# First loads in a fixed order on one queue with tiny transfers between them, four free places for weights, and eight products of zeros at the start of a two-layer trunk

## The chip, the core and the metric

One core of a Trainium2 chip runs the whole program. The engines are named as the profile names them: PE (TensorE, matrix products; PEld is its weight load), DVE (VectorE), ACT (ScalarE), POOL (GpSimd) and SP (SyncE, which issues all DMAs here). The metric is the device time of one execution in microseconds (us). It is the median of several runs. The span of the profile is the time from the first to the last instruction of one profiled execution, and it is a little shorter than the time of that execution.

## What is computed

The reference is a trunk of two layers on 256 positions of width 1024, in float32. Layer 0 mixes positions by a gated unit, layer 1 by attention with 16 heads; each is followed by a layer norm, a gated feed-forward part with a short convolution, and another layer norm. Only the very start is touched by the change:

```
def chunked_gmlp(x, w_in, ln_g, ln_b, w_s, b_s, w_out):
    z = jax.nn.gelu(x @ w_in)
    u, v = jnp.split(z, 2, axis=-1)
    v = layer_norm(v, ln_g, ln_b)
...
    sv = jnp.einsum('gts,bnsgc->bntgc', w, v) + b_s.T[None, None, :, :, None]
    return (u * sv.reshape(B, S, GMLP_WIDTH)) @ w_out
```

The kernel computes the half `v` first (weights `a_v`), then `u` (`a_u`), then the product with `w_out` (`a_out`). Everything after that is the same in both kernels but for small shifts in order.

## The kernel before

All weights come from DRAM in chunks of 128 x 2048 float32, which is 1 MB each. A chunk is loaded into one of two buffers `raw` and is split there: ACT writes a rounded copy `whi` (line 338) and DVE the remainder `wlo` (line 344), in halves of 1024 columns; both kinds have room for five chunks. The input `x` is treated in the same way: its transposed form `xT` is loaded to a place in `ff` and split into the two parts of `xt`. A product of two float32 matrices is then three products on PE: rounded by rounded, rounded by remainder, remainder by rounded (`mms`, line 326).

The first stage is `a_v`: four chunks, each with the weights of two of the eight input blocks k. For each k there are two row tiles t and two column halves, so 2 x 2 x 3 = 12 products of 512 columns, 96 in all. For k = 0 to 3 both row tiles take turns (48 products); then row tile 0 takes k = 4 to 7, then row tile 1. The second stage `a_u` has eight groups of 24 products of 256 columns, and mixed in are the small products of `spatial` (tiles `twos<-ff`), which need the normed `v`.

The order of the work is not written out. The code records operations with their dependences, and `Plan.emit` runs a model of the engines and issues each engine's instructions in the order of that model. Loads all go on SP's queue, in the order that the model gives; the first ones carry a rank, which the model uses as their due time. SP takes its instructions strictly in order, and one that waits for a buffer holds up all that stand behind it.

At the start chunk 0 is loaded in three pieces (512, 512 and 1024 columns) and chunk 1 in two (1024 each), mixed with `xT` in pieces of 1, 1, 2 and 4 blocks. `xT` lies in DRAM as partition, row tile, k, column, so a load of one block reads two runs of 128 elements in each partition. Chunks 2 and 3 go into the same two `raw` buffers as chunks 0 and 1, so each load waits until DVE has read the last half of the chunk before it. `lnrow` is a buffer of one chunk's size that holds the rows of a layer norm; its first use is the norm of `v`.

## Time and profile before

| what | value |
|---|---|
| median of 3 runs | 573.56 us |
| lowest and highest | 572.23 and 574.41 us |
| the profiled execution | 573.82 us |
| its span in the profile | 572.1 us |
| PE busy | 557.8 us (98%) |
| DVE busy | 459.9 us (80%) |
| ACT busy | 356.0 us (62%) |
| chain that ended last | PE 91%, DMA 4%, DVE 2%, SP's queue 1% |

PE is the engine of this kernel: what it does not spend on products is the start, the end and the few stretches where it waits. The groups of rows further down show the start closely. In the rows of the order of time, several instructions of one group that follow each other stand in one row (x2, x4), with the start of the first and the time from there to the end of the last; in square brackets stands how long the engine had been idle and what ended it. An idle time that ends with "DMA raw<-in_a_v" ends when such a load has landed.

### The profile page before, as it was taken

How to read it: one execution, taken by the hardware profiler on the slowest of the kernel's cores; microseconds unless marked ns; L12 is line 12 of the kernel's file. 1: busy time of each engine (PE TensorE's matmuls, PEld its weight loads, DVE VectorE, ACT ScalarE, POOL GpSimd, SP SyncE). 2: the span in 40 equal slices, each digit the busy share in tenths (PEclk: the TensorE clock that was granted, in tenths of full speed). 3: DMA queues.
4: the chain of work that ended last, by engine and by line, in shares of the span. 5: the costliest groups of instructions: out<-in, count | busy, mean ns of one | idle time of the engine just before them, and what ended most of it. 6: DMA issues, size and time to landing. Idle time of an engine off the chain costs nothing.

```text
span 572.1 us, 8555 instructions
## 1 busy us (share of the span) xinstructions
PE 557.8 (98%) x3226; PEld 482.7 (84%) x3226; DVE 459.9 (80%) x857; ACT 356.0 (62%) x652; POOL 11.5 (2%) x17
## 2 busy tenths in 40 slices
PE   6999999999999999999999999999999999999994
PEld 4799888888888878888899998788888888888884
DVE  4589989999999998467858767589989999997426
ACT  5474558776677786335569666367867767785300
POOL 0020010000000000001000000000000000000001
PEclk9999999999999999999999999999999999999998
DMA  7887644537554657652666542506456446566302
GB/s 259 307 300 288 257 147 158 211 147 255 187 220 149 221 224 263 227 212 92 221 221 236 207 156 84 222 1 211 158 215 226 183 186 214 196 245 231 144 1 73
DMA packets 20133, 110.93 MB, mean 194 GB/s; under 512 B 2251, under 2 KB 6268, under 8 KB 7676
## 3 DMA queue, kind: packets, MB, share of 16 engines
q1 hardware_dynamic: 20092, 110.39, 52.9%
q8 instruction: 25, 0.41, 0.3%
q14 instruction: 16, 0.13, 0.1%
HBM read 109.31 MB, written 1.07 MB: 193 GB/s over the span
## 4 chain that ended last, share of the span: by engine, by line
PE 91%; DMA 4%; DVE 2%; SPq 1%; ACT 0%; issue 0%; DVEq 0%
PE twos L326 52%; PE bank L326 38%; DMA raw<-in_a_v 2%; DMA raw<-in_a_u 2%; DVE wlo L344 1%; PE bank L332 1%; PE twos L332 1%; SPq L355 1%; ACT whi L338 0%; DVE x L348 0%; DVE ff L348 0%; DVE stat L494 0%; DVEq L964 0%; DVE stat L497 0%; DVE stat L499 0%
## 5 line engine op out<-in xcount | busy, mean ns | idle before, releaser
L344 DVE TENSOR_TENSOR wlo<-raw,whi 128x1024 fp32r<-128x1024 f32 (+1 forms) x212 | 228.9, 1103 | 39.2 <-ACT whi L338 38.6
L338 ACT ACTIVATE whi<-raw 128x1024 fp32r<-128x1024 f32 (+1 forms) x212 | 194.8, 954 | 58.7 <-DMA raw<-in_f_dn 24.5
L326 PE MATMUL twos<-xt,whi 128*128 128x512 f32 x640 | 222.2, 394 | 0.0
L326 PE MATMUL twos<-xt,wlo 128*128 128x256 f32 x640 | 177.3, 277 | 0.0
L326 PEld LDWEIGHTS twos<-xt,whi 128*128 128x128 f32 x640 | 120.0, 188 | 27.7
L326 PE MATMUL bank<-whi,rr 128*128 128x512 f32 x432 | 135.1, 391 | 0.0
L326 PEld LDWEIGHTS twos<-xt,wlo 128*128 128x128 f32 x640 | 120.2, 188 | 0.1
L326 PEld LDWEIGHTS bank<-whi,rr 128*128 128x128 f32 x432 | 81.1, 188 | 17.8 <-issue 1.0
L326 PE MATMUL bank<-wlo,rr 128*128 128x512 f32 x216 | 84.1, 389 | 0.0
L326 PE MATMUL bank<-xt,whi 128*128 128x256 f32 x384 | 71.8, 288 | 0.0
L348 DVE SCALAR_TENSOR_TENSOR ff<-ff,convc 128x254 f32<-128x254 f32 (+1 forms) x160 | 69.7, 478 | 0.5 <-ACT ff L338 0.2
L326 PEld LDWEIGHTS bank<-xt,whi 128*128 128x128 f32 x384 | 59.6, 191 | 2.0 <-issue 1.0
L338 ACT ACTIVATE ff<-twos 128x512 f32<-128x512 f32 (+1 forms) x56 | 31.0, 567 | 46.3 <-PE twos L326 43.9
L326 PE MATMUL bank<-xt,wlo 128*128 128x256 f32 x192 | 54.2, 282 | 0.0
L326 PEld LDWEIGHTS bank<-wlo,rr 128*128 128x128 f32 x216 | 40.6, 188 | 8.2
L338 ACT ACTIVATE ff<-ff,convc 128x256 f32<-128x256 f32 x80 | 45.6, 592 | 1.9 <-DVE ff L344 1.4
L326 PE MATMUL twos<-whi,xt 128*128 128x512 f32 x128 | 42.0, 396 | 0.0
L344 DVE TENSOR_TENSOR ff<-twos,ff 128x512 f32<-128x512 f32 (+1 forms) x48 | 30.9, 645 | 13.2 <-ACT ff L338 12.3
L338 ACT ACTIVATE ff<-bank,lncol 128x128 f32<-128x128 f32 x48 | 18.8, 458 | 30.5 <-PE bank L332 30.5
L326 PEld LDWEIGHTS bank<-xt,wlo 128*128 128x128 f32 x192 | 36.7, 191 | 0.0
L348 DVE SCALAR_TENSOR_TENSOR x<-x,bank 128x512 f32<-128x512 f32 x16 | 11.0, 686 | 27.4 <-PE bank L326 27.4
L326 PEld LDWEIGHTS twos<-whi,xt 128*128 128x128 f32 x128 | 24.1, 188 | 4.7
(70 smaller groups left out, 480.4 us busy)
## 6 DMA issues: line engine op xcount, KB each, us to landing
raw<-in_f_up SPq DMA_DIRECT2D x44, 1024.0 KB, 4.8
raw<-in_f_dn SPq DMA_DIRECT2D x22, 1024.0 KB, 4.8
raw<-in_b_qk SPq DMA_DIRECT2D x8, 1024.0 KB, 4.8
lnrow<-in_lnrow SPq DMA_DIRECT2D x5, 1024.0 KB, 5.8
raw<-in_a_u SPq DMA_DIRECT2D x4, 1024.0 KB, 4.7
raw<-in_a_out SPq DMA_DIRECT2D x4, 1024.0 KB, 5.1
raw<-in_b_v SPq DMA_DIRECT2D x4, 1024.0 KB, 4.8
raw<-in_b_o SPq DMA_DIRECT2D x4, 1024.0 KB, 4.8
```

The costliest lines, as they stand in the source:

```text
L326: nc.tensor.matmul(o, l, x, start=start, stop=stop)
L332: nc.tensor.transpose(o, x, ident.ap)
L338: plan.op("act", ns, lambda: nc.scalar.activation(o, x, func, **kw), r, w, table=table)
L344: dve(70 + 1.04 * flat(x), lambda: nc.vector.tensor_tensor(o, x, y, op=op), r, w)
L348: lambda: nc.vector.scalar_tensor_tensor(o, x, s, y, op0=op0, op1=op1), r, w)
L355: plan.op("sp", nbytes / 360.0, lambda: nc.sync.dma_start(o, src), r, w, nbytes=nbytes, rank=rank)
```

## The change

Five things are changed, all of them in the first stage.

- `xT` lies in DRAM so that the part of each partition that one load takes is one run: 256 elements for one block where there were two runs of 128. Both row tiles of up to two blocks are now split by one instruction each.
- Chunk 2 goes to a place in `ff` that is free at that time and chunk 3 to `lnrow`; neither waits for a `raw` buffer any more. The first norm's rows and `wsT` are loaded after these have been split.
- Ranked loads are issued strictly in the order of rank. Ahead of those with rank 5, 7, 9 and 10 stands a transfer of 16 elements from a loaded piece to `scratch`. It waits until the piece has landed, and since it stands on the same queue, what is behind it waits with it. The pieces are the first 512 columns of chunk 0, its second half, the first half of chunk 1 and its second half.
- DVE fills 512 columns with zeros at the start, and PE multiplies them eight times, into a bank that is used later.
- The twelve products of k = 0 are ordered so that both row tiles use a rounded half before its remainder, in the first column half and then in the second.

```diff
+WARM = 8
...
+                if e == "sp" and ranked:
+                    c = [x for x in c if x[1] is ranked[-1]]
...
+    FIRST = {0: [(0, 512, 0), (512, 1024, 2), (1024, 2048, 4)], 1: [(0, 1024, 6), (1024, 2048, 7)],
+             2: [(0, 2048, 9)], 3: [(0, 2048, 10)]}
...
     XFIRST = ((0, 1, 1), (1, 1, 3), (2, 2, 5), (4, 4, 8))
+
+    EARLY = {2: lambda: place("ff", HALF + KT * S, CH), 3: rowring.new}
+
+
+    HOLD = {5: (0, 0), 7: (0, SUB), 9: (1, 0), 10: (1, SUB)}
+    scratch = sb.tile([1, 16 * len(HOLD)], F32, name="scratch")
+    loaded, gates = {}, []
+
+    def hold(rank):
+        i, at = HOLD[rank]
+        g = Buf(scratch[:, 16 * len(gates):16 * len(gates) + 16])
+        load(g.ap, loaded[i].ap[:1, at:at + 16], [g], [(loaded[i], [at // 256])], nbytes=64, rank=rank - 0.5)
+        gates.append(g)
...
-        raw = raws.new()
+        raw = loaded[i] = EARLY.get(i, raws.new)()
         cuts = FIRST.get(i, [(0, CH, None)])
         for s, e, rank in cuts:
-            load(raw.ap[:, s:e], a[name][c, :, s:e], [(raw, range(s // 256, e // 256))], rank=rank)
+            if rank in HOLD:
+                hold(rank)
+            load(raw.ap[:, s:e], a[name][c, :, s:e], [(raw, range(s // 256, e // 256))],
+                 gates[-1:] if i <= CHUNKS else (), rank=rank)
...
+    zeros, idle = place("rr", 0, HALF), bank()
+    dve(480, lambda: nc.vector.memset(zeros.ap.bitcast(F32), 0.0), (), [zeros])
+    for _ in range(WARM):
+        mms([(idle.ap, zeros.ap[:, :P], zeros.ap, True, True)], [zeros], [idle], fill=True)
...
+        def first_step():
+
+            (hi, lo), x = sub("a_v", 0, 0), [at(0, t) for t in range(NT)]
+            for p in range(2):
+                for part, w in ((0, hi), (1, hi), (0, lo)):
+                    for t in range(NT):
+                        o, n, b = pieces[t][p]
+                        mms([(b.ap, x[t][part], w.ap[:, o:o + n], part == 0 and w is hi, False)],
+                            x[t][2][part:part + 1] + [(w, range(o // 256, (o + n) // 256))], [b])
+            plan.tick()
...
-        "xT": f(x.reshape(NT, P, KT, P).transpose(3, 0, 2, 1)),
+        "xT": f(x.reshape(NT, P, KT, P).transpose(3, 2, 0, 1).reshape(P, KT * S)),
```

On SP's queue, before, behind the first two 512-column pieces of chunk 0 and the first two blocks of `xT`, the loads stand like this (`raw_85` and `raw_86` are the two `raw` buffers):

```order
L355 DMA raw_85<-in_a_v 128x1024
L355 DMA ff<-in_xT 128x2x256
L355 DMA raw_86<-in_a_v 128x1024 x2
L355 DMA ff<-in_xT 128x2x512
L355 DMA raw_85<-in_a_v 128x2048
L355 DMA raw_86<-in_a_v 128x2048
L355 DMA lnrow_90<-in_lnrow 128x2048
L355 DMA raw_85<-in_a_u 128x2048
L355 DMA raw_86<-in_a_u 128x2048
```

And now at the same place:

```order
L361 DMA raw_85<-in_a_v 128x1024
L361 DMA scratch<-raw_85 1x16x1
L361 DMA ff<-in_xT 128x512
L361 DMA raw_86<-in_a_v 128x1024
L361 DMA scratch<-raw_85 1x16x1
L361 DMA raw_86<-in_a_v 128x1024
L361 DMA ff<-in_xT 128x1024
L361 DMA scratch<-raw_86 1x16x1
L361 DMA ff<-in_a_v 128x2048
L361 DMA scratch<-raw_86 1x16x1
L361 DMA lnrow_90<-in_a_v 128x2048
L361 DMA raw_85<-in_a_u 128x2048
```

Four tiny transfers stand between the loads, chunks 2 and 3 go to `ff` and `lnrow`, and the first load of `lnrow`'s own rows has moved behind two chunks of `a_u`.

On PE, before, the program starts with the products of k = 0 (`whi_65` and `wlo_75` are the parts of its weights, the four banks are the two row tiles by the two column halves):

```order
L326 MATMUL bank_107<-whi_65,xt 128x512
L326 MATMUL bank_107<-wlo_75,xt 128x512
L326 MATMUL bank_107<-whi_65,xt 128x512
L326 MATMUL bank_108<-whi_65,xt 128x512
L326 MATMUL bank_108<-wlo_75,xt 128x512
L326 MATMUL bank_108<-whi_65,xt 128x512
```

And now:

```order
L332 MATMUL bank_107<-rr 128x512 x8
L332 MATMUL bank_108<-whi_65,xt 128x512
L332 MATMUL bank_110<-whi_65,xt 128x512
L332 MATMUL bank_108<-whi_65,xt 128x512
L332 MATMUL bank_110<-whi_65,xt 128x512
L332 MATMUL bank_108<-wlo_75,xt 128x512
L332 MATMUL bank_110<-wlo_75,xt 128x512
```

The eight products of zeros stand first, and four products with `whi_65` come ahead of the first with `wlo_75`.

On PE in the second stage, before, the first products of `spatial` (`twos<-ff`) stand at the end of the third group of `a_u` (bank_109):

```order
L326 MATMUL bank_109<-xt,whi_65 128x256 x2
L326 MATMUL bank_109<-xt,wlo_75 128x256
L326 MATMUL twos_105<-ff 128x128 x2
L326 MATMUL twos_106<-ff 128x128 x2
L326 MATMUL bank_110<-xt,whi_66 128x256 x2
```

And now they stand behind the first three products of the third group (bank_110 there):

```order
L332 MATMUL bank_109<-xt,whi_74 128x256 x2
L332 MATMUL bank_109<-xt,wlo_84 128x256
L332 MATMUL bank_110<-xt,whi_65 128x256 x2
L332 MATMUL bank_110<-xt,wlo_75 128x256
L332 MATMUL twos_105<-ff 128x128 x2
L332 MATMUL twos_106<-ff 128x128 x2
L332 MATMUL bank_110<-xt,whi_65 128x256 x2
```

They have moved forward by 21 of the group's 24 products.

## Rows read from the trace of the kernel before

**Rows 1.** The page: the span, and the engines' shares of the chain that ended last.

```profile
span 572.1 us, 8555 instructions
...
PE 91%; DMA 4%; DVE 2%; SPq 1%; ACT 0%; issue 0%; DVEq 0%
```

**Rows 2.** All waits of PE in the whole span: total us, times, longest.

```profile
PE bank L326 <- DVE xt L361: 5.0, 1, 5.0
PE bank L326 <- DVE wlo L344: 1.3, 2, 0.8
PE twos L326 <- DVE ff L348: 0.2, 1, 0.2
```

**Rows 3.** PE in order of time, first stage: start us, time us, what. The last row is the first product of the second stage.

```profile
5.00 0.77 PE L326 MATMUL bank<-whi,xt 128*128 128x512 f32 x1 [5.00 <-DVE xt L361]
5.85 0.79 PE L326 MATMUL bank<-wlo,xt 128*128 128x512 f32 x1
...
8.57 0.63 PE L326 MATMUL bank<-wlo,xt 128*128 128x512 f32 x1
...
11.13 0.54 PE L326 MATMUL bank<-wlo,xt 128*128 128x512 f32 x1
11.51 0.62 PE L326 MATMUL bank<-whi,xt 128*128 128x512 f32 x2
...
13.35 0.39 PE L326 MATMUL bank<-wlo,xt 128*128 128x512 f32 x1
...
14.03 0.39 PE L326 MATMUL bank<-wlo,xt 128*128 128x512 f32 x1
...
19.02 0.61 PE L326 MATMUL bank<-whi,xt 128*128 128x512 f32 x2
20.21 0.50 PE L326 MATMUL bank<-wlo,xt 128*128 128x512 f32 x1 [0.58 <-DVE wlo L344]
...
24.04 0.50 PE L326 MATMUL bank<-wlo,xt 128*128 128x512 f32 x1 [0.76 <-DVE wlo L344]
...
32.11 0.40 PE L326 MATMUL bank<-xt,whi 128*128 128x256 f32 x2
```

**Rows 4.** Stretches: busy us (instructions) of PE, PEld, DVE, ACT and POOL, then the granted clock, the share of the DMA engines and GB/s.

```profile
5.00:7.00 2.00, 1.92 (x4) 1.22 (x5) 1.69 (x4) 0.63 (x1) 0.00 (x0) 1.00 0.85 240
...
10.00:11.00 1.00, 1.00 (x4) 0.81 (x3) 0.90 (x2) 0.54 (x3) 0.00 (x0) 1.00 1.01 412
...
35.00:40.00 5.00, 5.00 (x44) 5.00 (x43) 5.00 (x12) 2.66 (x4) 1.71 (x2) 1.00 0.89 344
```

**Rows 5.** ACT in order of time: the splits of `raw` and `xT` and the loads that ended its waits.

```profile
4.29 0.63 ACT L338 ACTIVATE whi<-raw 128x512 fp32r<-128x512 f32 x1 [2.21 <-DMA raw<-in_a_v]
5.46 0.63 ACT L338 ACTIVATE whi<-raw 128x512 fp32r<-128x512 f32 x1 [0.54 <-DMA raw<-in_a_v]
7.46 0.51 ACT L338 ACTIVATE xt<-ff 128x128 fp32r<-128x128 f32 x2 [1.37 <-DMA ff<-in_xT]
8.94 1.15 ACT L338 ACTIVATE whi<-raw 128x512 fp32r<-128x512 f32 x2 [0.97 <-DMA raw<-in_a_v]
10.56 0.72 ACT L338 ACTIVATE xt<-ff 128x256 fp32r<-128x256 f32 x2 [0.46 <-DMA ff<-in_xT]
11.85 2.42 ACT L338 ACTIVATE whi<-raw 128x512 fp32r<-128x512 f32 x4 [0.57 <-DMA raw<-in_a_v]
14.41 1.15 ACT L338 ACTIVATE xt<-ff 128x512 fp32r<-128x512 f32 x2
17.84 2.01 ACT L338 ACTIVATE whi<-raw 128x1024 fp32r<-128x1024 f32 x2 [2.27 <-DMA raw<-in_a_v]
21.67 2.01 ACT L338 ACTIVATE whi<-raw 128x1024 fp32r<-128x1024 f32 x2 [1.83 <-DMA raw<-in_a_v]
```

**Rows 6.** DVE in order of time at the start.

```profile
0.87 0.06 DVE L421 MEMSET nhalf<- 128x1 f32 x1 [0.87 <-PEq L961]
4.63 0.36 DVE L361 CAST xt<-ff 128x128 fp32r<-128x128 f32 x2 [3.70 <-DMA ff<-in_xT]
5.11 0.68 DVE L344 TENSOR_TENSOR wlo<-raw,whi 128x512 fp32r<-128x512 f32 x1
```

**Rows 7.** SP's queue in order of time: when a load was issued. The last row is a piece of the chain that ended last: the fourth `a_u` chunk, from its issue to its landing.

```profile
3.16 0.60 SPq L355 DMA_DIRECT2D raw<-in_a_v  x1
...
10.93 4.51 SPq L355 DMA_DIRECT2D raw<-in_a_v  x2
...
35.92 4.74 DMA raw<-in_a_u
```

**Rows 8.** The second stage in order of time: ACT's gelu of `v`, DVE's norm of `v` with a split of weights in it, and the wait of the first `spatial` products on PE.

```profile
33.46 1.07 ACT L338 ACTIVATE ff<-bank 128x512 f32<-128x512 f32 x2
...
35.82 1.87 DVE L494 BATCH_NORM_STATS2 stat<-ff 128x6 f32<-128x512 f32 x3
...
39.67 1.22 DVE L344 TENSOR_TENSOR wlo<-raw,whi 128x1024 fp32r<-128x1024 f32 x1
40.81 0.48 DVE L348 SCALAR_TENSOR_TENSOR ff<-ff,stat,lnrow 128x256 f32<-128x256 f32 x1
...
40.74 0.39 PE L326 MATMUL twos<-ff 128*128 128x128 f32 x2
41.35 0.94 PE L326 MATMUL twos<-ff 128*128 128x128 f32 x6 [0.22 <-DVE ff L348]
```

More of the change, by code (lines that the diff above doesn't have):

```diff
@@ L156, in emit @@
         nb = 0
+        ranked = sorted((o for o in ops if o.rank is not None), key=lambda o: -o.rank)
         def ready(o):
@@ L188, in emit @@
             cand[e].remove(pick)
+            if o.rank is not None:
+                ranked.remove(o)
             if o.eng == "pe" and not o.fill:
@@ L379, in trunk_kernel @@
     chunks = {}
-    FIRST = {0: [(0, 512, 0), (512, 1024, 2), (1024, 2048, 4)], 1: [(0, 1024, 6), (1024, 2048, 7)]}
+    FIRST = {0: [(0, 512, 0), (512, 1024, 2), (1024, 2048, 4)], 1: [(0, 1024, 6), (1024, 2048, 7)],
+             2: [(0, 2048, 9)], 3: [(0, 2048, 10)]}
     XFIRST = ((0, 1, 1), (1, 1, 3), (2, 2, 5), (4, 4, 8))
+    EARLY = {2: lambda: place("ff", HALF + KT * S, CH), 3: rowring.new}
[7 more added lines that the diff above has]
+        gates.append(g)
     def prep(i):
         name, c = stream[i]
-        raw = raws.new()
+        raw = loaded[i] = EARLY.get(i, raws.new)()
         cuts = FIRST.get(i, [(0, CH, None)])
         for s, e, rank in cuts:
-            load(raw.ap[:, s:e], a[name][c, :, s:e], [(raw, range(s // 256, e // 256))], rank=rank)
+            if rank in HOLD:
+                hold(rank)
+            load(raw.ap[:, s:e], a[name][c, :, s:e], [(raw, range(s // 256, e // 256))],
+                 gates[-1:] if i <= CHUNKS else (), rank=rank)
         subs = []
@@ L430, in trunk_kernel, with cut @@
     xT32 = place("ff", HALF, KT * S)
-    xv32 = xT32.ap.rearrange("p (t k c) -> p t k c", t=NT, k=KT)
     def load_xt(k, n, rank):
-        load(xv32[:, :, k:k + n, :], a["xT"][:, :, k:k + n, :], [(xT32, [(t, j) for t in range(NT) for j in range(k, k + n)])],
-             rank=rank)
-        for t in range(NT):
-            parts = [(t, j) for j in range(k, k + n)]
-            split((xh, parts, xt_view(xh)[:, t, k:k + n, :]), (xl, parts, xt_view(xl)[:, t, k:k + n, :]),
-                  (xT32, parts, xv32[:, t, k:k + n, :]), by="dve" if k == 0 else "act")
-    prep(0)
-    for k, n, rank in XFIRST:
-        load_xt(k, n, rank)
-    for i in range(1, CHUNKS):
+        def cut(j, m):
+            return slice(j * S, (j + m) * S), [(t, i) for t in range(NT) for i in range(j, j + m)]
+        sl, parts = cut(k, n)
+        if rank in HOLD:
+            hold(rank)
+        load(xT32.ap[:, sl], a["xT"][:, sl], [(xT32, parts)], gates[-1:], rank=rank)
+        for j in range(k, k + n, 2):
+            m = min(2, k + n - j)
+            sl, parts = cut(j, m)
+            hv, lv = (both[:, j:j + m, o:o + S] for o in (0, S))
+            xv = xT32.ap[:, sl].rearrange("p (k x) -> p k x", k=m)
+            split((xh, parts, hv), (xl, parts, lv), (xT32, parts, xv), by="dve" if k == 0 else "act")
+    zeros, idle = place("rr", 0, HALF), bank()
+    dve(480, lambda: nc.vector.memset(zeros.ap.bitcast(F32), 0.0), (), [zeros])
+    for _ in range(WARM):
+        mms([(idle.ap, zeros.ap[:, :P], zeros.ap, True, True)], [zeros], [idle], fill=True)
+    prep(0)
+    for x in XFIRST[:3]:
+        load_xt(*x)
+    prep(1)
+    load_xt(*XFIRST[3])
+    for i in range(2, CHUNKS):
         prep(i)
@@ L645, in gmlp @@
         v = []
+        def first_step():
[7 more added lines that the diff above has]
+            plan.tick()
         for k, t in order:
+            if k == 0:
+                if t == 0:
+                    first_step()
+                continue
             rows_step(pieces[t], *at(k, t), *sub("a_v", k // 2, k % 2), k == 0, k == KT - 1)
```

## The prediction

> **What bounds the kernel now.** I read the page first, then PE's waits, then the start in order of time. The page [rows 1] says that PE makes up 91% of the chain that ended last. The list of waits [rows 2] is short: 5.0 us for the first operand, 1.3 us in two waits for a split of weights, 0.2 us in one wait for the norm of `v`. After that PE waits for nothing to the end, so this change can gain only in the first stage and at that last wait, and what it gains there stays if nothing behind gets late.
>
> The first stage lasts from 5.00 to 32.11 [rows 3], 27.1 us for 96 products. At the stage's own best pace (three products from 13.35 to 14.03, 0.227 us each) they would take 21.8 us. The other 5.3 us are these:
>
> - Slow steps. From 8.57 to 11.13 six products take 2.56 us, 0.427 us each, which is 512 columns at 1.2 GHz; later it is 0.227 us, the level of 2.4 GHz. The clock column reads 1.00 there too [rows 4], so for this stretch the steps tell the level. The level rises at about 11.4, which is 6.4 us after the first product. 13 slow products lose 0.20 us each, and one step of 0.38 in the change loses 0.15: 2.75 us.
> - Two waits at the first products of chunks 2 and 3. From 19.02 to 20.21 stand two steps and a wait of 0.74 us; the wait before 24.04 is longer (idle 0.76 against 0.58). With slower first steps behind each they make up what the other two items leave of the 5.3, some 1.95 us. Both end on DVE's split, but the split is late because the load is: it is issued at 10.93, once the buffer is free [rows 7], and lands at 17.8 and 21.7 [rows 5].
> - At k = 0, seven products take from 5.00 to 8.57, 3.57 us where seven steps are 2.99: 0.58 us of waits for the remainders.
>
> **The early clock.** The zeros have to be filled first. DVE is free from 0.93; a fill of one column took 0.06 and a full pass over 512 columns 0.68 [rows 6], so it ends between 1.0 and 1.6, and I take 1.5 for the first product of zeros. Eight slow steps are 3.4 us, so they end at 4.4 to 5.1; the first real operands are there at 5.0, as before, since the first weights (landed at 4.3, plus 0.63 for ACT's split [rows 5]) and the first `xT` are not held. The eight products thus cost 0 to 0.1 us. No row shows a product of zeros; if PE treats them as any other, the level rises 6.4 us after 1.5, at 7.9.
>
> **Weights of k = 1.** With a faster PE these come next. Before, they landed at 8.94, behind a 128 KB piece of `xT` that took 2.0 us (5.46 to 7.46) [rows 5]. A piece of 512 KB of weights took 1.29 us (10.56 to 11.85), 406 GB/s, at which the 128 KB would take 0.32 us. The slow stretch shows it too: 240 GB/s at 5 to 7 against 412 at 10 to 11, with the DMA engines 0.85 busy [rows 4]. With runs twice as long the excess of 1.68 us may go wholly or not at all: the weights land between 7.26 and 8.94. I take the middle, 8.1, since the number of runs is halved. The next piece of `xT` (256 KB) has an excess of 0.97 (8.94 to 10.56 is 1.62 us, 0.65 at full rate), and the half of both is 1.3 us for all loads behind.
>
> **The first stage, put together.** PE starts at 5.0. Two products with `whi` go to 5.85; the remainder of `xT` is ready near 5.95, behind DVE's split of the first weights (4.63 + 0.36 + 0.68 + 0.3), so 0.1 us is lost; five more slow steps reach 8.1 and five fast ones 9.2. The k = 1 weights are split by ACT at 8.1 + 0.63 = 8.7 and by DVE at 9.4, and the second product asks for the latter at 9.4: no wait. Twelve products at 0.227 end at 11.95, the other 72 at 28.3, if none waits.
>
> Do they wait? Chunk 2 is asked for behind k = 2 and 3, at 11.95 + 5.45 = 17.4. Before, all loads ahead of it had landed by 14.4 [rows 5]; minus 1.3 that is 13.1, plus 2.6 for 1 MB at 406 GB/s 15.7, plus the time in which the holds let the queue run dry. That has no row. A dry queue costs at most its latency: 4.74 us from issue to landing of 1 MB [rows 7], minus 2.6, is 2.2; with two issues ahead of it (0.60 for a load [rows 7], and 0.3 for the tiny transfer, an estimate at half of that), 3.1 us for each hold. Against this stands what is already queued behind the piece that is waited for: 1 MB (2.6 us), 768 KB (1.9), 1 MB (2.6) and 1.5 MB (3.9). So the four holds cost at most 0.5 + 1.2 + 0.5 + 0 = 2.2 us, and nothing if the slowest DMA engine, which makes the landing, is never the dry one. I take 0.6. Chunk 2 then lands at 16.3, its parts are ready at 16.9 and 17.6, and PE asks for them at 17.4 and 17.6. Chunk 3 lands at 18.9, is split behind chunk 2 by 19.6 and 20.2, and is asked for at 20.1. The margins are thin, and the two waits before 20.21 and 24.04 are gone but for a tenth or two.
>
> Sum: clock 2.75 to 1.4, which is 1.35; chunks 1.95; k = 0 0.58 to 0.1, which is 0.48; together **3.8 us** off the first stage (32.11 to 28.3).
>
> **The second stage.** What is queued behind SP's waits: the first `a_u` chunks follow chunk 3 at once and land near 21.5 and 24.1, four us before PE asks for the first. `lnrow`'s rows wait for chunk 3's split (20.8) and `wsT` and two chunks of `a_u` stand behind it; those are asked for 11 us after the stage begins. The norm of `v` is the late one: its first `spatial` products now stand 21 products earlier. Three groups took from 32.11 to 40.74, 2.88 us each [rows 3, 8], so PE asks at 28.3 + 5.8 + 0.4 = 34.5. Before, DVE had the operand ready at 41.3, since ACT's gelu stood behind a split until 33.46 and DVE began the statistics only at 35.82; from there it took 5.5 us, 1.2 of them a split (39.67) that now stands behind [rows 8]. With the `a_u` chunks landed at 24.1 those splits are done when `v` is; gelu ends at 29.3, DVE begins at 28.9 and is done 4.3 us later, 33.2. So the margin is 1.3 us and the 0.2 us of wait there may go as well; I count nothing for it. Larger `xT` splits and the fill of zeros on DVE lie in its idle time ahead of 5 us and at 14 to 18, and cost nothing; without that cover each would cost at most the 0.68 us of a full pass [rows 6].
>
> The profiled execution took 573.82 us, 1.7 over its span, and its sum is 570.0; the median of the runs is 0.26 lower, so I forecast 573.56 - 3.8 = **569.8**.
>
> **The rivals.**
>
> - *The zeros don't lift the clock.* Then it rises 6.4 us after 5.0 as before. The gain keeps the chunks and k = 0, less what is thus no longer in the way: PE does k = 0 to 10.4, k = 1 with three slow products to 13.6, the rest to 29.9. Gain 2.2, 571.3. For it speaks that no row shows such a product; against it that all 14 products up to 11.13 are equal in form to those behind and only the time sets them apart, so nothing in the rows points to what is multiplied.
> - *The holds let the queue run dry.* With all of the 2.2 us chunk 2 lands at 17.9, the remainder is ready at 19.2 instead of 17.6, and PE waits 1.6 us: gain 2.2, 571.4. For it: four waits for a landing on the queue that has everything behind it; against it: 768 KB or more is always queued. The Trainium skill (DMA: Bandwidth & Descriptors, Rules for kernel authors) says to issue a DMA early and to wait on it late, which speaks against these holds; by that rule this rival's 571.4 is the outcome, and no row here shows a queue held on purpose.
> - *The norm of `v` isn't moved forward.* Place: the first `spatial` products on PE, now ahead of 21 others that covered the wait. DVE is busy all of 35 to 40 [rows 4]. If its chain ended at 41.3 as before, PE would stand from 34.5 on, 6.8 us; against the gain of 3.8 and the 0.2 us of before this is 2.8 us slower, 576.4. It decides from an operand later than 38.3. Against it stand the earlier `a_u` loads; for it that ACT and DVE take their work strictly in order, so one late split of `a_u` ahead of gelu moves the whole chain. A delay of half that size gives 573.0, no change.
> - *More than forecast.* The `xT` pieces come at full rate and the clock rises before 6: k = 0 ends at 8.3, k = 1 at 11.05, the stage at 27.4, gain 4.7, 568.9; with the 0.2 us wait and some 0.3 of earlier first operands 568.4.
>
> **How the numbers follow.** Forecast 0.60 (569.3 to 570.6), more than forecast 0.10, zeros without effect 0.11, dry queue 0.11, the norm 0.08, of which half slower than before. The first of these and the stronger gain are faster by over 0.5% (below 570.7; 0.5% is about what a measurement of this kernel can tell from no change), with a few hundredths from the two rivals near 571.3: faster 0.70, within 0.5% 0.26, slower 0.04. The range holds the forecast, the stronger gain and the rivals at 571.3 and 571.4 and the scatter of a median of some 0.5 us: 568.3 to 572.0.
>
> **What would show it.** Right: eight products into a bank from about 1.5 at 0.427 us steps; steps of 0.227 from about 8; the `whi` split of k = 1 starting near 8.1; no wait of PE longer than 0.3 us after 6; the first product of `a_u` at 28.3; `spatial` near 34.5 without a wait. Wrong: steps of 0.427 up to 11; PE idle at the first product of chunk 1, 2 or 3, with a wait that ends on a load; a DMA rate that falls to nothing between 8 and 13; the first `spatial` products ended by DVE after 36.

## The result, and the profile after

The changed kernel takes **579.99 us**, the median of 6 runs (577.93 to 580.92), against 573.49 us (572.23 to 574.41) for the kernel before on the same chip: a ratio of 1.0124 with a 95% interval of 1.0105 to 1.0143. It is slower by 6.5 us where 3.8 us less were forecast, and far outside the range. The profiled execution took 580.25 us.

First the page of the changed kernel, span and chain, beside [rows 1], and then all waits of PE, beside [rows 2] (us in total, times, longest).

```profile
span 578.5 us, 8568 instructions
...
PE 94%; DMA 3%; ACT 1%; DVE 1%; SPq 0%; issue 0%; DVEq 0%
```

```profile
PE bank L338 <- ACT ff L344: 2.1, 4, 0.6
PE bank L332 <- ACT whi L344: 1.6, 1, 1.6
PE bank L332 <- DVE nhalf L445: 1.5, 1, 1.5
PE twos L332 <- ACT xt L344: 0.9, 1, 0.9
PE bank L332 <- DVE xt L350: 0.3, 1, 0.3
PE bank L332 <- DVE wlo L350: 0.2, 1, 0.2
```

The wait of 5.0 us at the start has become one of 1.5, since the zeros come first. The waits for `wlo` and for the norm of `v` are nearly gone, one for chunk 2 (1.6) has come. The first and the fourth line are new and belong to no step of the forecast. They are not the whole of the loss: these two lines name 3.0 us, and the span has grown by 6.4.

The start, in order of time, beside [rows 3]: start, time, what. The last row is again the first product of the second stage.

```profile
1.52 3.74 PE L332 MATMUL bank<-rr 128*128 128x512 f32 x8 [1.52 <-DVE nhalf L445]
5.09 0.64 PE L332 MATMUL bank<-whi,xt 128*128 128x512 f32 x2
5.98 0.73 PE L332 MATMUL bank<-whi,xt 128*128 128x512 f32 x2 [0.25 <-DVE xt L350]
...
7.01 1.09 PE L332 MATMUL bank<-whi,xt 128*128 128x512 f32 x4
...
8.39 0.39 PE L332 MATMUL bank<-whi,xt 128*128 128x512 f32 x1
...
17.34 0.39 PE L332 MATMUL bank<-whi,xt 128*128 128x512 f32 x1
19.35 0.50 PE L332 MATMUL bank<-whi,xt 128*128 128x512 f32 x1 [1.62 <-ACT whi L344]
20.07 0.50 PE L332 MATMUL bank<-wlo,xt 128*128 128x512 f32 x1 [0.22 <-DVE wlo L350]
...
31.14 0.40 PE L332 MATMUL bank<-xt,whi 128*128 128x256 f32 x2
```

The zeros start at 1.5 as forecast and are gone by 5.1. From 7.01 to 7.94 four products take 0.23 us each, so the clock is already at its upper level there. But the stage ends at 31.14, not at 28.3: PE stands before the first product of chunk 2. ACT's splits, beside [rows 5], show which loads are late; then SP's queue, beside [rows 7], with the tiny transfers (`scratch`); then two windows, beside [rows 4] (busy us and instructions of PE, PEld, DVE, ACT, POOL; granted clock; DMA share; GB/s).

```profile
7.46 1.15 ACT L344 ACTIVATE whi<-raw 128x512 fp32r<-128x512 f32 x2 [0.88 <-DMA raw<-in_a_v]
...
13.52 1.15 ACT L344 ACTIVATE whi<-raw 128x512 fp32r<-128x512 f32 x2 [1.81 <-DMA raw<-in_a_v]
14.72 1.15 ACT L344 ACTIVATE xt<-ff 128x512 fp32r<-128x512 f32 x2
18.67 2.19 ACT L344 ACTIVATE whi<-ff 128x512 fp32r<-128x512 f32 x4 [2.79 <-DMA ff<-in_a_v]
21.63 2.19 ACT L344 ACTIVATE whi<-lnrow 128x512 fp32r<-128x512 f32 x4 [0.77 <-DMA lnrow<-in_a_v]
```

```profile
10.61 0.50 SPq L361 DMA_DIRECT2D scratch<-raw  x1
11.15 0.58 SPq L361 DMA_DIRECT2D ff<-in_a_v  x1
13.51 0.50 SPq L361 DMA_DIRECT2D scratch<-raw  x1
```

```profile
5.00:7.00 2.00, 1.75 (x7) 1.15 (x7) 1.62 (x4) 0.94 (x2) 0.00 (x0) 1.00 0.96 317
10.00:11.00 1.00, 1.00 (x6) 0.84 (x5) 0.60 (x1) 0.45 (x1) 0.00 (x0) 1.00 0.91 233
```

The weights of k = 1 are there at 7.46 (8.94 before). The rate at 5 to 7 has risen from 240 to 317 GB/s, but at 10 to 11 it has fallen from 412 to 233; two holds have gone before. All loads ahead of chunk 2 have landed at 14.7, no earlier than before (14.4), and chunk 2 lands at 18.65, held until 11.15.

Where the rest went is seen when the same product is looked up in both traces. The table gives the start of the changed kernel's product less that of the one before. The stages have the names of their weights, as in the kernel: behind `a_out` come the feed-forward parts of the two layers (`f_up0` and `f_dn0`, `f_up1` and `f_dn1`), with the attention (`b_v` to `b_o`) between them. Most of an `f_up` stage is a stream of pairs: one product of 512 columns with `whi` and one of 256 with `wlo`, 640 products in a stage.

| up to | after minus before, us | in this stretch |
|---|---|---|
| end of a_v, [rows 3] | -0.97 | -0.97 |
| after the spatial stage (55 us) | -1.74 | -0.77 |
| end of a_out (78) | -1.73 | 0.01 |
| 16 products into the pairs of f_up0 (98) | -0.29 | **+1.44** |
| end of these pairs (208) | +1.79 | **+2.08** |
| end of f_dn0 (270) | +1.85 | 0.06 |
| b_v (284) | +3.02 | **+1.17** |
| end of b_o (381) | +3.03 | 0.01 |
| 16 products into the pairs of f_up1 (401) | +4.51 | **+1.48** |
| end of these pairs (511) | +6.58 | **+2.07** |
| last product | +6.64 | 0.06 |

So in these two profiles the start gained 1.7 us, three places between stages lost 4.1, and the two long stages of pairs lost 4.15. How much of the 1.7 belongs to the change is settled by more profiles of the kernel before (e4 below). At the first of the three places, the transposes ahead of f_up0, PE in the kernel before and then in the changed one:

```profile
85.77 0.60 PE L332 MATMUL bank<-ident,x 128*128 128x128 f32 x4
...
86.91 0.60 PE L332 MATMUL bank<-ident,x 128*128 128x128 f32 x4
...
90.10 0.60 PE L332 MATMUL bank<-ident,ff 128*128 128x128 f32 x4
```

```profile
86.08 1.04 PE L338 MATMUL bank<-ident,x 128*128 128x128 f32 x8
87.63 0.44 PE L338 MATMUL bank<-ident,ff 128*128 128x128 f32 x2 [0.51 <-ACT ff L344]
88.63 0.44 PE L338 MATMUL bank<-ident,ff 128*128 128x128 f32 x2 [0.56 <-ACT ff L344]
```

Before, products stand between the two groups of four and twelve more ahead of the next transposes, so that ACT's copies are done when PE comes. Now all eight stand together and the dependent ones right behind them, and PE waits for ACT. The same is seen at 276 us, where products with `xt` are the dependent ones, and at 389. The change touches no line there; the small shifts in order, of which the text ahead of the prediction speaks, are these.

In the pairs PE waits for nothing. The products by form from 110 to 200 us, before and then after (count, busy us, mean ns of one):

```profile
L326 PE MATMUL twos<-xt,whi 128*128 128x512 f32 x261 | 90.5, 394 | 0.0
L326 PE MATMUL twos<-xt,wlo 128*128 128x256 f32 x260 | 72.0, 277 | 0.0
```

```profile
L332 PE MATMUL twos<-xt,whi 128*128 128x512 f32 x256 | 90.5, 399 | 0.0
L332 PE MATMUL twos<-xt,wlo 128*128 128x256 f32 x256 | 71.9, 281 | 0.0
```

In the same 90 us four to five pairs fewer are issued. The steps from start to start repeat over three pairs in the changed kernel, over two in the one before:

```
after:   236 113 232 118 241 120 ns   3 pairs in 1.060 us, 60 products in 10.60
before:  230 113 232 118 ns           2 pairs in 0.693 us, 60 products in 10.40
```

Over the 640 products of a stage the difference is 2.1 us. The granted clock is 1.00 in both. From here on the two are called the slow and the fast pace.

The kernel before has the slow steps too, at the start of each of its `f_up` stages. The last of its first three pairs in f_up0 has steps of 0.24 and 0.12 us, then come four transposes, and behind them its pairs are fast:

```profile
95.36 0.40 PE L326 MATMUL twos<-xt,whi 128*128 128x512 f32 x1
95.60 0.28 PE L326 MATMUL twos<-xt,wlo 128*128 128x256 f32 x1
95.72 0.60 PE L332 MATMUL bank<-ident,ff 128*128 128x128 f32 x4
```

All 28 `f_up` stages of the 14 profiles start like this: the pairs begin with the slow steps (227 113 233 117 241 120 ns), four such transposes come in between after three pairs (after six in f_up1 of the changed kernel, e5, e6, e9 and e11), and what follows them, slow or fast, then lasts to the end of the stage or to the next disturbance.

### The profile page after: what moved, and what is told of

Read it like the earlier page. It is cut to its first block, busy times and chain, and to the rows that moved or that the text cites. A ratio compares the mean times of both kernels' runs of the same rounds, so it can differ in the third digit from the quotient of the medians.

```text
span 578.5 us, 8568 instructions
## 1 busy us (share of the span) xinstructions
PE 564.3 (98%) x3234; PEld 485.0 (84%) x3234; DVE 459.2 (79%) x858; ACT 358.7 (62%) x654; POOL 10.2 (2%) x17
## 4 chain that ended last, share of the span: by engine, by line
PE 94%; DMA 3%; ACT 1%; DVE 1%; SPq 0%; issue 0%; DVEq 0%
PE twos L332 52%; PE bank L332 41%; DMA raw<-in_a_v 1%; DMA ff<-in_a_v 1%; PE twos L338 1%; PE bank L338 1%; ACT ff L344 1%; DVE x L354 0%; SPq L361 0%; ACT ff L803 0%; ACT xt L344 0%; DVE wlo L350 0%; ACT whi L344 0%; DVE stat L532 0%; DVEq L1018 0%
## 5 line engine op out<-in xcount | busy, mean ns | idle before, releaser
L350 DVE TENSOR_TENSOR wlo<-raw,whi 128x1024 fp32r<-128x1024 f32 (+1 forms) x208 | 224.5, 1097 | 42.5 <-ACT whi L344 41.9
L332 PE MATMUL twos<-xt,whi 128*128 128x512 f32 x640 | 226.4, 399 | 0.0
L344 ACT ACTIVATE whi<-raw 128x1024 fp32r<-128x1024 f32 (+1 forms) x208 | 191.1, 957 | 55.7 <-PE bank L332 26.0
L332 PE MATMUL twos<-xt,wlo 128*128 128x256 f32 x640 | 179.7, 281 | 0.0
L354 DVE SCALAR_TENSOR_TENSOR ff<-ff,convc 128x254 f32<-128x254 f32 (+1 forms) x160 | 67.4, 478 | 1.2 <-ACT ff L344 1.2
L344 ACT ACTIVATE ff<-ff,convc 128x256 f32<-128x256 f32 x80 | 44.0, 594 | 14.4 <-DVE ff L350 14.3
L332 PE MATMUL twos<-whi,xt 128*128 128x512 f32 x128 | 40.8, 392 | 0.9 <-ACT xt L344 0.9
```

Of the source, the lines that this page charges most:

```text
L332: nc.tensor.matmul(o, l, x, start=start, stop=stop)
L344: plan.op("act", ns, lambda: nc.scalar.activation(o, x, func, **kw), r, w, table=table)
L350: dve(70 + 1.04 * flat(x), lambda: nc.vector.tensor_tensor(o, x, y, op=op), r, w)
L354: lambda: nc.vector.scalar_tensor_tensor(o, x, s, y, op0=op0, op1=op1), r, w)
```

## The experiments

Each ran beside the kernel before on the same chip; ratios are to that, with 95% intervals.

**First set: the reordered transposes.** The order is not written out but worked out by the `Plan`, which simulates all engines. It takes due times from PE's work without stalls, and lets an engine wait for a more urgent operation only if that ends before the due time of the one at hand. Each hold is charged there as a load that waits for a landing, with the next load waiting for it in turn. The times that the plan works out for PE end at 543.0 us for the changed kernel, at 530.8 for the one before. Theory A: this lateness alone reorders the transposes.

*e1: no holds.*

```
-    HOLD = {5: (0, 0), 7: (0, SUB), 9: (1, 0), 10: (1, SUB)}
+    HOLD = {}
```

> The changed kernel without its four tiny transfers, neither on the queue nor in the plan; strict order, free places, zeros and the new first step stay. Theory A (the holds are charged in the plan's model, the model runs some 12 us later, and from that lateness on it groups the transposes ahead of three later stages so that PE waits): the three waits on ACT near 88, 278 and 390 us are gone, the first stage is not worse, and the time falls from 580.0 to 570 to 573. Theory B (another part of the change costs the time: the zeros, the places, the larger splits): 578 to 581 with the same waits. Theory C (the pairs of products in the two f_up stages take 0.353 us in place of 0.347 for a reason of their own, such as the eight more products on PE): the waits are gone but the pairs stay slow, 574 to 576.

573.15 us, 1.0015 (1.0002 to 1.0029). The plan ends at 530.7, and the transposes stand as before. No wait over 0.2 us is left behind 50 us, and the pairs are at the fast pace (394 and 277 ns). The start gains nothing: without holds the k = 1 weights land at 10.11 us, between the large loads. PE waits, and the clock falls. PE's row of the wait, then windows behind it (columns as above):

```profile
10.82 0.51 PE L332 MATMUL bank<-whi,xt 128*128 128x512 f32 x1 [2.12 <-ACT whi L344]
```

```profile
11.00:12.00 1.00, 0.78 (x3) 0.42 (x4) 1.00 (x2) 0.81 (x2) 0.00 (x0) 1.00 1.06 434
12.00:13.00 1.00, 1.00 (x4) 0.73 (x3) 0.69 (x3) 0.66 (x2) 0.00 (x0) 0.53 1.01 422
13.00:15.00 2.00, 2.00 (x6) 1.61 (x5) 2.00 (x4) 1.75 (x4) 0.00 (x0) 0.50 1.05 440
```

The a_v stage ends at 32.12, so the first stage is worse than the changed kernel's (31.14), which was not expected. The holds thus bring the weights of k = 1 forward, 7.4 instead of 10.1; the forecast had counted the larger runs alone for this. The larger runs without holds show no gain: e1's rate at 5 to 7 us is 249 GB/s (240 before), and its loads ahead of chunk 2 have landed at 14.86 (14.38 before). Its chunk 2 lands at 17.36, ahead of the changed kernel's 18.65.

*e2: the holds stay on the queue, but the plan counts them as nothing.*

```
-            if e == "sp":
+            if e == "sp" and o.nbytes == 64:
+                o.end = free[e] = s
+            elif e == "sp":
...
-        load(g.ap, loaded[i].ap[:1, at:at + 16], [g], [(loaded[i], [at // 256])], nbytes=64, rank=rank - 0.5)
+        load(g.ap, loaded[i].ap[:1, at:at + 16], [g], (), nbytes=64, rank=rank - 0.5)
```

> The changed kernel with its four tiny transfers on the queue as they are, but free of charge and of dependences in the plan's model. Theory A (only the model's lateness costs): the order of the later stages is that of before, their waits are gone, 571 to 574, with a first stage as long as the changed kernel's. Theory B' (the holds themselves cost on the chip, by a queue that runs dry): 578 or more. Between A and no_holds the difference is what the holds cost on the queue: by A 0 to 2 us, in the first stage alone.

572.51 us, 1.0001 (0.9983 to 1.0019). On the chip each hold still waits for its chunk; only the plan does not know of it. The transposes stand as before, the late waits are gone, and the pairs are fast. Chunk 2 lands at 19.25, PE waits 2.12 us for it at 19.96, the clock falls to the lower level from 21.4 to 24.9, and a_v ends at 33.12, not with the changed kernel as Theory A expected. Since the other edits of the change stay in e1 and e2, these do not cause the loss behind 80 us.

*e3: the kernel before, with 9 us added to all clocks of the plan behind the 200th product.*

```
+                if nb == 200:
+                    free = {x: f + 9000.0 for x, f in free.items()}
+                    bus += 9000.0
```

> The kernel before, where the plan's model is set 9 us later for all engines and the bus at the 200th group of products; no instruction is added, the first stages are word for word those of before, the order near 88 us too, and the transposes near 278 and 390 us are grouped as in the changed kernel. Theory A: two waits of some 1.2 us come back and nothing else in the start, 575.5 to 576.5; if the slow pairs in f_up follow from that order, those of the second f_up stage (after 390 us) are slow too and those of the first are not, 577.5 to 578.5. Theory B: 573.5, no change.

574.66 us, 1.0045 (1.0026 to 1.0063), a little less than the 575.5 that was expected at least. Nothing of the work or of the start is changed, and the waits come, +1.16 us near 278 and +1.46 near 390. Two of PE's waits:

```profile
PE bank L335 <- ACT ff L341: 1.1, 2, 0.6
PE twos L329 <- ACT xt L341: 0.9, 1, 0.9
```

The transposes near 86 us kept their order here, so lateness alone is shown to move them at two places of the three. The pairs stay at 10.40 in both stages, one of which follows reordered transposes: the slow pace is a thing of its own.

*e4: the kernel before, again.*

> The kernel before once more, unchanged. If the pace of the pairs in the f_up stages is fixed by the program, both stages run at 0.693 us for two pairs as in the profile before and the time is 573.5 within 0.3%; if it differs from run to run, one of the stages shows 1.060 us for three pairs (some 2 us more in that stage) in this profile, and the runs scatter by 2 us or more.

571.95 us, 0.9995 (0.9982 to 1.0007). Its first stage ends at 30.91, where the steps fall to 0.227 us at 9.4 instead of 11.5:

```profile
30.91 0.40 PE L326 MATMUL bank<-xt,whi 128*128 128x256 f32 x2
```

The profile on which the forecast rests was thus one of the slower starts. Four profiles have the start of the kernel before and end a_v at 32.11, 30.91, 31.04 (e3) and 30.61 (e10), 31.17 in the mean; four have the start of the changed kernel and end it at 31.14, 32.11 (e5), 30.45 (e9) and 31.59 (e11), 31.32 in the mean. The 0.77 us of the spatial stage in the table are not the change's either: from the end of a_v to the product at 55 us it takes 24.2 us in the changed kernel and in e3, e4 and e10 alike, and only the profile before shows 24.95, with its wait of 0.22 for the norm. So no gain of the start is shown.

**Second set: which part, and whose is the slow pace?**

*e5: the changed kernel, again.*

> The changed kernel once more, nothing edited. Theory C1 (the slow pace of the pairs in the two f_up stages belongs to this program: where its instructions stand, or their order): both stages again take 10.60 us per 60 products, the span is again 577.5 to 579 us and the ratio to before 1.010 to 1.014. Rival C2 (the pace is drawn anew in each execution): in one or both stages the profile shows 10.40 us per 60, and the span is 2.4 or 4.8 us shorter, 573.5 to 576.5. Whichever holds, the later waits (two of 0.5 us for the ff split by ACT near 88 and 391 us, one of 0.9 near 278) come again, since the order of the instructions is fixed.

578.74 us, 1.0117 (1.0091 to 1.0142). All late waits are there again. The pairs ran at 10.60 in f_up0 and at 10.40 in f_up1: the same program shows both paces, and C1 as it stands has fallen. C2 holds in so far.

*e6: the changed kernel without products of zeros.*

```
-WARM = 8
+WARM = 0
```

> The changed kernel with no products of zeros (the fill of the zeros by VectorE stays). The order of every other instruction is as in the changed kernel, so Theory A (the holds, charged in the plan, put later transposes into a bad order) expects the later waits as there: some 1.1 to 1.3 us each near 86, 278 and 390 us. The clock should rise some 5 us after the first real product, near 9.4 to 11.4 us, instead of 5.1; that costs 13 to 20 slow products, 2.6 us at most, of which the wait for chunk 2 (1.6 us) swallows a part: the end of a_v at 31.1 to 33. If the zeros are worth nothing (rival), 31.1. Slow pairs: if it is the position of the pairs in the program that sets the pace, eight products fewer may give the fast pace, and the span is 4.8 us shorter (573 to 575); if it is the order of the transposes together with the plan, the pace stays slow (578 to 580).

578.15 us, 1.0112 (1.0092 to 1.0132), and a_v ends at 31.01 (31.14 with zeros). So the zeros gain nothing here, the rival of the expectation. Steps fall to 0.23 us at 8.5, and what is lost there is regained at chunk 2, where PE waits 1.3 us instead of 1.6. The pace is fast in f_up0, slow in f_up1.

*e7: the two first holds alone.*

```
-    HOLD = {5: (0, 0), 7: (0, SUB), 9: (1, 0), 10: (1, SUB)}
+    HOLD = {5: (0, 0), 7: (0, SUB)}
```

> The changed kernel with the two holds of the xT piece and of the second half of chunk 1 alone; chunks 2 and 3 are not held. Both holds are charged in the plan as in the changed kernel; its own end lies 3 us behind the one of before instead of 12, and the transposes of the three later stages stand as in before. Theory A expects no later waits and fast pairs, so the whole gain of the start stays: k = 1 weights at 7.3 to 7.5 as in the changed kernel, chunk 2 no later than without holds (17.4) or 1 us later, asked for at about 17, wait 0.3 to 1.3 us, end of a_v at 29 to 30.5, time 0.5 to 2 us below before: ratio 0.996 to 0.999. Theory B' (a hold as such delays what comes after, however it is planned): chunk 2 lands at 18.6 or later, a_v ends at 31 or later, ratio 1.000 to 1.002. Theory B (another part of the change makes the later waits): the waits near 86, 278 and 390 us come back, ratio 1.005 or more.

575.34 us, 1.0062 (1.0044 to 1.0080). The time misses Theory A's 0.996 to 0.999 and looks like Theory B, but the trace does not: the plan ends at 533.9, the transposes stand apart, and the late waits are gone. a_v ends at 30.05, chunk 2 lands at 17.79 (18.65 with all holds). The loss is in the pairs, both stages at 10.60, 2.07 us each, so the fast pairs that Theory A expected did not come. f_up0 from 110 to 200 us:

```profile
L332 PE MATMUL twos<-xt,whi 128*128 128x512 f32 x255 | 90.1, 399 | 0.0
L332 PE MATMUL twos<-xt,wlo 128*128 128x256 f32 x256 | 71.9, 281 | 0.0
```

*e8: the kernel before with the zeros alone.*

```
+    zeros, idle = place("rr", 0, HALF), bank()
+    dve(480, lambda: nc.vector.memset(zeros.ap.bitcast(F32), 0.0), (), [zeros])
+    for _ in range(8):
+        mms([(idle.ap, zeros.ap[:, :P], zeros.ap, True, True)], [zeros], [idle], fill=True)
```

> The kernel before with the eight products of zeros added and nothing else. The forecast's step on the clock expects a rise near 5 us, so the 13 slow products up to 11.4 (2.75 us) shrink; but the weights of k = 1 land at 8.9 as before and are split by 9.6 to 10.3, so PE waits there some 1 to 1.5 us, and chunk 2 lands at 17.8 as before: end of a_v 30 to 31.5, ratio 0.997 to 0.999, and pairs at the fast pace, since the later order is that of before. Rival: the gain of the clock is wholly given back to waits for loads, or the clock falls again in such a wait: a_v ends at 31.5 or later, ratio 0.999 to 1.002. Second rival: the zeros shift all later pairs by eight instructions and bring the slow pace: ratio 1.005 to 1.009.

571.83 us, 0.9998 (0.9986 to 1.0010). In the profile a_v ends at 29.82, 1.1 us earlier than in e4; over 12 runs no gain is left that can be told from none. The pairs are fast. From 55 us on until after f_up0, PE's products stand in the same order in e7 (slow) and e8 (fast).

**Third set: is the pace a phase?** In the pairs, one 512-column product is now and then issued as two of 256 columns, with the same operands and result. Nothing else moves.

```
-                nc.tensor.matmul(o, l, x, start=start, stop=stop)
+                if cut and flat(x) == HALF:
+                    for j in range(2):
+                        nc.tensor.matmul(o[:, j * S:(j + 1) * S], l, x[:, j, :] if len(x.shape) == 3 else x[:, j * S:(j + 1) * S],
+                                         start=start, stop=stop)
+                else:
+                    nc.tensor.matmul(o, l, x, start=start, stop=stop)
```

*e9: the changed kernel, nine cuts in each stage.*

> The changed kernel; in each of the two f_up stages nine of the 512-column products of the pairs (one in every second group of 32 products, at a different place of the group each time) are issued as two of 256 columns, with the same operands and the same result. The order of all else is that of the changed kernel. Each cut adds one product and costs some 0.01 to 0.15 us, 18 of them 0.2 to 2.7 us. Theory D (the pace of the pairs is a phase that locks behind a disturbance and then repeats): behind some of the cuts the pace changes inside a stage; both paces, 10.40 and 10.60 us per 60, are seen in one execution, and if most cuts end in the fast one the span is 2 to 4.8 us shorter less the price of the cuts. Rival E (the pace belongs to the stage of this program, by operands, traffic or placement): every stretch between cuts runs at 10.60 and the span is that of the changed kernel plus the price of the cuts. The later waits for the reordered transposes come as in the changed kernel under both.

579.87 us, 1.0150 (1.0117 to 1.0184); the profiled execution took 578.43.

*e10: the kernel before, the same cuts.*

> The kernel before with the same 18 cuts, nothing else. Theory D: since each cut is a new draw of the phase, some stretches run at 10.60 per 60 although the kernel before has shown only 10.40 so far; the time is before plus 0.2 to 2.7 us for the cuts plus 0.12 us for every group that falls to the slow pace. Rival E: all stretches stay at 10.40, and the time is before plus the price of the cuts.

573.09 us, 1.0026 (1.0013 to 1.0039). Theory D holds: both kernels show both paces within one stage, and behind the four transposes the pace changes at a cut and nowhere between. Steps of e9 in f_up1 around two cuts; the fast pace has a second pattern there, 230 117, of the same length:

```
... 230 117 230 117 [118 117] 118 235 113 233 117 241 120 236 113 233 117 241 ...   fast to slow
... 241 120 236 113 233 117 [121 120] 124 235 117 235 116 230 117 230 117 230 ...   slow to fast
```

The outcome is regular: in the slow pace, a cut of the product with the step of 241 ended in the fast one each time (6 of 6), a cut of the other two never (all nine cuts of f_up0 in e9 fell on those). The kernel before gets slow stretches by cuts alone. A cut costs next to nothing: f_up0 of e9, slow throughout, lost 2.14 us with nine cuts, 2.08 in the changed kernel without. That e9's span would fall, if most cuts ended in the fast pace, did not come true: its cuts left f_up0 slow, and in f_up1 four of the nine ended in the slow pace.

*e11 and e12: one cut in each stage, on the product with the step of 241; in the changed kernel, and in e7.*

```
-                cols_apart(b, j * HALF, h, l, *sub(name, i, j))
+                cols_apart(b, j * HALF, h, l, *sub(name, i, j), 4 if (i, j) == (3, 0) else None)
```

> The changed kernel with one 512-column product cut into two of 256 columns in each f_up stage, near its start: the fifth pair of the second group of 16 pairs, which in the slow pace is the one with the step of 0.241 us. Theory D, from the cuts before: a cut of that product (step 0.241) ended in the fast pace in every case, one of the other two phases (0.236, 0.232) in none. So if the stage starts slow, as in the changed kernel, the pairs run at 10.60 us per 60 up to the cut and at 10.40 behind it, in both stages; some 610 products are left behind each cut, so 2.0 us a stage, 4.0 us together: span 574 to 575, median 574.5 to 576.5, ratio 1.004 to 1.008, and what is left over before is the later waits. Where a stage starts fast the cut may also turn it slow, and then 2 us are missing. Rival E' (a cut changes the pace only by chance): the paces behind this cut are mixed, and the time stays above 577.

577.99 us, 1.0118 (1.0105 to 1.0131). The time alone would be that of Rival E'; the steps decide for Theory D. f_up0 was slow up to the cut and turned fast behind it. f_up1 was already fast ahead of the cut in this execution, as in e5, and the cut turned it slow. So the profiled execution has one slow stage, not none, which the expectation had named as the case in which 2 us are missing. The 512-column products of e11 from 110 to 200 and from 400 to 500 us:

```profile
L337 PE MATMUL twos<-xt,whi 128*128 128x512 f32 x260 | 90.2, 392 | 0.0
```

```profile
L337 PE MATMUL twos<-xt,whi 128*128 128x512 f32 x284 | 100.3, 399 | 0.0
```

> The kernel with the two first holds alone (e7) and the same cut. It has no later waits, and its pairs were slow in both stages. Theory D: both stages turn fast behind the cut, 4.0 us less than the 575.34 of e7: 571 to 572, ratio 0.997 to 1.001, which would be the start of the changed kernel (the end of a_v at 30 as in e7) at no loss behind. Rival E': the pace stays slow in one stage or both: 573 to 575.5, ratio 1.002 to 1.006.

571.52 us, 0.9999 (0.9990 to 1.0008), 3.8 us below e7, which ran on another chip; by the ratios it is 3.6. Both stages turned fast; the same two stretches:

```profile
L337 PE MATMUL twos<-xt,whi 128*128 128x512 f32 x261 | 90.5, 391 | 0.0
```

```profile
L337 PE MATMUL twos<-xt,whi 128*128 128x512 f32 x290 | 100.6, 391 | 0.0
```

Two products split in two took the loss away, as forecast by Theory D. What stays of the start in e12 (a_v ends at 29.51, chunk 2 without a long wait) is no faster than the kernel before: against e4 the 1.4 us of a_v shrink to 0.5 behind the spatial stage, where PE waits 0.5 us for the norm of `v`, and to 0.2 at the end. No version here beats the kernel before.

## Why the prediction was wrong

**The step that failed** is in its first paragraph: that what the start gains "stays if nothing behind gets late". The part on the second stage then looked only as far as `spatial`, at 41 us. Two things behind cost 8.2 us. And the gain itself, the sum of 3.8 us for the first stage, did not come: 0.97 us in the pair of profiles, nothing over four profiles of either start.

1. *The plan is part of the kernel* (4.1 us, three places). The forecast named the queue behind each hold on the chip, but not what charging a hold does to the plan. Lateness of some 12 us in its own reckoning moved transposes at 86, 276 and 389 us to right ahead of what needs them. Shown by e1, e2 and e7 (no such lateness, no such waits) and by e3 (lateness alone, the waits). That the rule on due times, told above, is what gives way is read from the code and was not tried; at 86 us lateness alone was not shown to do it. The order of both kernels could be compared beforehand and shows the moved transposes; the forecast did not look there.

2. *The pace of the pairs* (4.15 us in the profile). The forecast took the pairs as given; the slow steps at the start of the `f_up` stages stand in the trace of the kernel before, but only for three pairs. Shown by e9 to e12: the pace is a phase of PE's stream of products that a disturbance sets and the stream then keeps. In the kernels as they are the disturbance is the four transposes after the first pairs. The step from the last product ahead of them to the first of the four goes with what follows: 119 or 120 ns in 13 of the 28 stages, all fast behind it; 121 to 123 in 11, of which ten were slow; 124 or 125 in 4, all fast. The kernels in which the holds are charged left the transposes slow in 10 of 14 stages (the changed kernel, e5, e6, e7, e9, e11, e12) and the others in none of 14 (before, e1 to e4, e8, e10). What makes the difference of these few ns stays open. Neither the order of PE's products (e7 and e8) nor the program as such (e5 shows both paces) decides it.

**The start**, forecast at 3.8 us, gave 0.97 at the end of a_v against the profile before, and against e4, the same kernel, it is 0.23 behind. Its terms:

- *Clock, 1.35*. Right that zeros lift it: the steps fall to 0.23 at 5.1 in the changed kernel (7.9 was forecast), at 4.4 to 7.7 in all with zeros, at 8.5 to 11.5 in those without. But the price was taken from the one profile with the latest rise, and a faster PE only comes earlier to a load that is not there. e6 (without zeros, same end of a_v) and e8 (zeros alone, ratio 0.9998) show nothing of this term in the time; by e8's interval it is 0.8 us at most. The zeros were free, as said.
- *Weights of k = 1*: forecast to land at 8.1, they did at 7.44, but not for the reason given. With the same larger runs and no hold they land at 10.11 (e1), so it is the holds that brought them forward, and that the number came near is luck.
- *Chunks 2 and 3, 1.95*: the term of the first stage that was mis-sized most. Chunk 2 was to land at 16.3 and landed at 18.65. e1 tells two parts of these 2.35 us apart. Without holds the forecast's sum is 15.7, and in e1, which has none, chunk 2 landed at 17.36: 1.7 us are not the holds'. They are the 1.3 us and more that the larger runs were to save on all loads and did not: the loads ahead of chunk 2 were to end at 13.1 and ended at 14.70, in e1 at 14.86, before at 14.38. The other 0.7 are the holds': chunk 2 landed at 17.36 with none, at 17.79 with two (e7), at 18.65 with four, so they cost 1.3 us where 0.6 was taken and 2.2 was the most. From the loads ahead to chunk 2 it took 3.95 us instead of the 2.6 of the bytes. So the rival *the holds let the queue run dry* names the smaller part; that its wait of 1.6 us at chunk 2 is met so closely is in part luck, since its chunk 2 lands at 17.9. The Trainium skill (DMA: Bandwidth & Descriptors, Rules for kernel authors) says to issue a DMA early and wait late; e7 agrees, where chunk 2, issued 1.9 us earlier without its hold, landed 0.86 us earlier. e1 is the other side: without any hold the weights of k = 1 are late.
- *k = 0, 0.48*: the operand came as forecast, the gain did not. The remainder of `xT` is there at 5.98 (5.95 was forecast). The twelve products take from 5.09 to 8.39, 3.3 us, where twelve fast steps are 2.7: the same 0.58 us are lost as before, since the faster PE comes to the remainders earlier.
- *The norm of `v`*: the rival in which it would be late did not come. The first `spatial` products start without a wait at 37.26, 6.1 us behind the end of a_v (6.2 was forecast). The 0.2 us of wait that might go as well are not there in e4 either. In e12, where the start is faster still, PE waits 0.5 us for the norm, a part of that rival.

The range was wrong because every rival lay within the first 41 us; the loss lies behind.

## What to carry to other kernels

Where an order is worked out by a model, an edit at the start can move instructions anywhere: compare the order of the two kernels to the end, and ask what the model charges for each new operation. Hold a load back only where the next operand is late: here the first two holds brought the weights of k = 1 forward (7.5 us against 10.1), and the last two only made chunk 2 later (18.65 against 17.79); neither shows in the time. Take the price of a start from more than one profile, since that of the kernel before ended its first stage anywhere from 30.6 to 32.1 us. A stage that runs without any wait can still lose 2%: count the instructions in equal stretches of both traces before looking for a wait.

## What the runs showed of the hardware

- Pairs of products of 512 and 256 columns have at least two steady paces on PE, 0.347 and 0.353 us a pair, at a granted clock of 1.00 with the same instructions; one cut product can switch between them. For comparison, the Trainium skill (TensorE: Matmul & The Clock Gate, Back-to-back issue gap) gives N / 2.4 + 2.5 ns as the isolated gap of a product of N columns at the upper level; by it a pair would take 0.325 us, an estimate from that page. Both measured paces are above it.
- In the first stage the clock fell to its lower level at the end of a wait of PE for a load of 2.0 to 2.1 us or shortly behind it: in e1 from 12.1 to 15.5, in e2 from 21.4 to 24.9, in e5 from 19.4 to 22.8, where the stage ended 1 us later than in the profile of the same program with a wait of 1.6 us and no fall.
- When the clock rises differs between executions of the same start: in the start of the kernel before, the steps fell at 8.9 (e10), 9.4 (e4), 10.3 (e3) and 11.5 us (before). One profile does not give this time for the kernel.
